# Differential attention in split float32: score matmuls on half the rows of TensorE, and score tiles in pairs of maps

## The chip, the cores and the metric

The kernel runs on one core of one Trainium2 chip. The metric is device time in microseconds (us) for one execution. The engines of the core work at the same time, each through its own instructions in order: TensorE (PE in the profile, PEld its weight loads), VectorE (DVE), ScalarE (ACT), GpSimd (POOL) and SyncE (SP), whose queue issues nearly all DMA transfers here.

## The reference

An encoder layer is applied to two requests, a prompt of 2048 tokens and a sample of 1024, with 1024 features in float32. One big projection gives the inputs of a convolution branch and of an attention branch; the two results are gated, added, projected and normalised. The change touches the attention only:

```python
def diff_attention(q, k, v, lam):            # q, k: (B, S, 4 heads, 2 maps, 64)
    ...
        s = jnp.einsum('bqhcd,bkhcd->bhcqk', q_blk, k).astype(jnp.float32) * scale
        p = jax.nn.softmax(s, axis=-1)
        a = p[:, :, 0] - lam * p[:, :, 1]
        return jnp.einsum('bhqk,bkhe->bqhe', a.astype(v.dtype), v)
```

Each head has two attention maps (c = 0 and 1), each with 64 features for queries and keys. Both go through a softmax, the second is taken from the first with a factor, and the difference multiplies the values.

## The kernel before

The kernel has three stages. Stage A projects and runs the convolution, stage B is the attention, stage C merges and projects. Spills between them go through DRAM.

TensorE's products are made from halves: a float32 number x is kept as a high half, x rounded to the format of the fast matmul (float32r), and a low half, the rest. Stage A writes both halves of queries and keys: `qd[g][h][0]` is high, `[1]` low, and rows 0 to 63 belong to map 0, rows 64 to 127 to map 1. In the names, g is 0 for the prompt and 1 for the sample, h is the head.

In stage B a `Head` (L460) holds the keys of a head in tiles `km[c, hf]` of 128 x 1024: for map c and the half hf of the keys, the high halves on rows 0 to 63 and the low ones on rows 64 to 127. A `Pair` (L476) is 256 queries of a head: 32 pairs in the prompt, 16 in the sample. It loads four query tiles `qq` (L489): for each map the high halves, once on the upper and once on the lower 64 rows, and the low halves in the same way, in eight loads. `score` (L495) makes one PSUM tile `s` of 128 queries (j is 0 or 1) by 1024 keys. It has four matmuls of 512 columns over all 128 rows (L505): the high queries, and then the low ones, against high and low keys together, so all four products of halves are in the sum. The eviction (L507, on VectorE) scales the tile into a buffer `e` and keeps its smallest value. PSUM holds two tiles `s`, two tiles `tp` and two tiles `ops`.

What follows for each j: `soften` (L511) is the exponential of a whole map on ScalarE (L518); `combine` (L521) a reciprocal on VectorE (L524) and three steps on GpSimd (L525 to L527) that bring both maps into one buffer `e`. `turn` (L528 to L537) transposes two blocks of 128 keys for both j, four matmuls into `tp` (L534), and ScalarE rounds them into `ah` (L536). `rest` (L539) takes the low half `al` on VectorE (L541). `product` (L544) makes six matmuls with the values (L95 to L97). After a pair's last product come the squares on ScalarE (`squares`, L551) and, for the pair before, their sum by two matmuls (`sums`, L566).

The order in stage B is written out by hand: TensorE, VectorE, ScalarE and GpSimd take their instructions as the loop at L596 issues them, and only SyncE's order is found by a scheduler. A pass of this loop, a slot below, issues at most one score tile with its eviction, then the turn of an earlier pair, then what stands in the list `mid` for this slot (exponentials, squares), then a product, `al`, and what stands in `late` (combine). So a steady slot on TensorE is four scores, four transposes, six products. A pair of the prompt takes eight slots of scores, and its turns begin eight slots after its last score (`LAGS`); a pair of the sample takes four. The prompt's first two pairs have no turns beside them. Up to `NE` = 8 buffers `e` exist, and `live` counts those in use: a score that needs a new one waits for its slot until the count allows it (L600). Every fourth slot also splits a piece of the weights that stage C keeps resident (L580, L581).

The order of the work in a j before the change is map 0 with both halves of the keys, then map 1 with both halves; the exponential of a map is issued in the slot after its last half.

## Time and profile before

| | |
|---|---|
| Time, median of 3 runs | 2825.17 us (2818.87 to 2825.88) |
| Span of the profiled execution, first to last instruction | 2816.1 us |
| Its own total | not given by the page; the span is 2.8 to 9.8 us under the three runs |
| TensorE busy, matmuls | 2709.3 us (96%), 13818 |
| VectorE, ScalarE, GpSimd busy | 1843.1, 1074.4, 1478.5 us (65%, 38%, 53%) |
| Score matmuls (L505) | 1280, from 1548.0 to 2227.1 us, 352.3 us busy |
| Evictions of scores (L507) | 320, 1.22 or 1.28 us each |

The shares are averages over three stages. Stage B runs from about 1548 to 2230 us, and what the change is worth is read there. In a row of a timeline stand the start, the duration, the engine, the line, the operation, the output and the inputs with their shapes, and how many instructions of a kind the row merges; in brackets the idle time of the engine ahead of it and what ended that. Matmuls overlap in the array, so the duration of a group is longer than its step to the next group. A row of the windows has, after the window and its length, for each engine the busy time and the number of instructions, then the granted clock of TensorE.

### The profile page before, as it was taken

To read this page: it belongs to the slowest core of one execution; us is meant where nothing else is said; L and a number is where in the kernel's file an instruction comes from. 1 tells how busy PE (TensorE), PEld (TensorE's weight loads), DVE (VectorE), ACT (ScalarE), POOL (GpSimd) and SP (SyncE) were. 2 spreads that over 40 slices of the span, in tenths; PEclk is the share of its full clock that TensorE was granted. 3 is DMA by queue.
4 is the path that set the end of the run, shared out by engine and by line. 5 is a ranking of instruction groups with operands and counts; after the bars stand their busy time and mean duration, and the time that the engine had idled before them with its cause. 6 is when DMAs were issued, how large, how long until landed. Compare 5 with 4: busy or idle time off the path is not lost. (4 is left out here: it accounts for less than half of the span.)

```text
span 2816.1 us, 36981 instructions
## 1 busy us (share of the span) xinstructions
PE 2709.3 (96%) x13818; PEld 2274.5 (81%) x13818; DVE 1843.1 (65%) x2564; ACT 1074.4 (38%) x1540; POOL 1478.5 (53%) x774
## 2 busy tenths in 40 slices
PE   9989999998999998979999999999999999999998
PEld 7868988887897877858878788888888877777777
DVE  4961110396387495994940888888888866667665
ACT  3122132212322222213121788878788822222121
POOL 3554232245535424546442899988888833333343
PEclk9999999999999999989999999999999999999999
DMA  6245323324443343334333332322234375566553
GB/s 194 71 152 179 126 105 112 143 72 158 157 142 119 108 138 104 105 127 156 105 116 112 109 85 88 85 69 70 69 94 116 104 253 190 182 207 200 181 162 119
DMA packets 194980, 364.89 MB, mean 130 GB/s; under 512 B 25088, under 2 KB 98288, under 8 KB 194800
## 3 DMA queue, kind: packets, MB, share of 16 engines
q1 hardware_dynamic: 193792, 362.22, 40.1%
q8 instruction: 109, 1.79, 0.3%
q14 instruction: 71, 0.58, 0.1%
q10 hardware_dynamic: 1008, 0.29, 0.1%
HBM read 242.67 MB, written 107.18 MB: 124 GB/s over the span
## 5 line engine op out<-in xcount | busy, mean ns | idle before, releaser
L127 POOL TENSOR_TENSOR wl<-raw,wh 128x1024 fp32r<-128x1024 f32 (+1 forms) x138 | 416.5, 3038 | 485.6 <-ACT wh L126 471.8
L291 PE MATMUL psA<-xh,wh 128*128 128x512 f32 x1920 | 600.6, 395 | 37.7 <-DVE ev L255 16.5
L159 DVE SCALAR_TENSOR_TENSOR acc<-uc,conv_dw,acc 128x512 f32<-128x512 f32 x720 | 608.5, 896 | 5.8
L291 PE MATMUL psA<-xl,wh 128*128 128x512 f32 x1920 | 598.6, 393 | 0.9 <-DVE xl L284 0.9
L291 PE MATMUL psA<-xh,wl 128*128 128x512 f32 x1920 | 597.7, 393 | 0.3 <-POOL wl L127 0.3
L291 PEld LDWEIGHTS psA<-xh,wh 128*128 128x128 f32 x1920 | 365.4, 191 | 116.9 <-DVE ev L255 17.8
L291 PEld LDWEIGHTS psA<-xl,wh 128*128 128x128 f32 x1920 | 365.4, 190 | 78.8 <-DVE xl L284 1.6
L291 PEld LDWEIGHTS psA<-xh,wl 128*128 128x128 f32 x1920 | 364.6, 190 | 77.6 <-POOL wl L127 1.0
L527 POOL TENSOR_TENSOR e<-e 128x2048 f32<-128x2048 f32 (+1 forms) x96 | 373.1, 3887 | 8.0
L505 PE MATMUL s<-km,qq 128*128 128x512 f32 x1280 | 352.3, 397 | 4.8 <-DVE e L507 4.4
L518 ACT ACTIVATE e<-e,mx 128x2048 f32<-128x2048 f32 (+1 forms) x192 | 329.5, 1716 | 1.2 <-DVE e L507 1.1
L507 DVE TENSOR_SCALAR_CACHE_REDUCE e<-s 128x1024 f32<-128x1024 f32 x192 | 233.4, 1216 | 77.1 <-PE s L505 75.7
L541 DVE TENSOR_TENSOR al<-tp,ah 128x512 fp32r<-128x512 f32 x320 | 220.1, 688 | 56.1 <-ACT ah L536 56.1
L505 PEld LDWEIGHTS s<-km,qq 128*128 128x128 f32 x1280 | 219.7, 189 | 41.3 <-DVE e L507 10.7
L126 ACT ACTIVATE wh<-raw 128x1024 fp32r<-128x1024 f32 (+1 forms) x138 | 134.0, 1012 | 285.0 <-PE psA L291 164.9
L536 ACT ACTIVATE ah<-tp 128x512 fp32r<-128x512 f32 x320 | 189.5, 593 | 98.7 <-PE tp L534 96.1
L90 POOL TENSOR_TENSOR zl<-zraw,zh 128x512 fp32r<-128x512 f32 x88 | 123.8, 1409 | 162.4 <-ACT zh L89 142.5
L95 PE MATMUL ops<-ah,vv 128*128 128x256 f32 x640 | 207.3, 324 | 0.2 <-ACT row L567 0.2
L534 PEld LDWEIGHTS tp<-ident,e 128*128 128x128 f32 x1280 | 158.6, 141 | 48.6 <-DVE al L541 3.7
L534 PE MATMUL tp<-ident,e 128*128 128x128 f32 x1280 | 193.3, 274 | 4.5 <-POOL e L527 3.0
L97 PE MATMUL ops<-al,vv 128*128 128x256 f32 x640 | 180.7, 282 | 0.7 <-DVE al L541 0.7
L96 PE MATMUL ops<-ah,vv 128*128 128x256 f32 x640 | 179.7, 281 | 0.0
(165 smaller groups left out, 4259.5 us busy)
## 6 DMA issues: line engine op xcount, KB each, us to landing
raw<-in_w_in SPq DMA_DIRECT2D x130, 512.0 KB
qq<-qd SPq DMA_DIRECT2D x384, 64.0 KB
zraw<-in_w_out SPq DMA_DIRECT2D x88, 256.0 KB
ev<-ev SPq DMA_DIRECT2D x96, 128.0 KB
kd<-ev SPq DMA_DIRECT2D x24, 512.0 KB
qd<-ev SPq DMA_DIRECT2D x24, 512.0 KB
vd<-ev SPq DMA_DIRECT2D x24, 512.0 KB
mcd<-evm SPq DMA_DIRECT2D x24, 512.0 KB
```

Source lines behind the costliest of these rows:

```text
L95: nc.tensor.matmul(ps, ah, bh, start=first, stop=False)
L97: nc.tensor.matmul(ps, ah, bl, start=False, stop=last)
L127: nc.gpsimd.tensor_sub(lo, raw, hi.bitcast(F32))
L159: nc.vector.scalar_tensor_tensor(acc[:, c], src, dw_sb[:, c, k:k + 1], acc[:, c], op0=ALU.mult, op1=ALU.add)
L291: nc.tensor.matmul(ps[:, n * 512:(n + 1) * 512], w[a][:, k, j * P:(j + 1) * P], B.xs[k][x][:, n * 512:(n + 1) * 512], start=k == 0 and a = ...
L505: nc.tensor.matmul(s[:, n * 512:(n + 1) * 512], p.qt[2 * c + i][:, j * P:(j + 1) * P], p.km[c, hf][:, n * 512:(n + 1) * 512], start=i == 0 ...
L507: nc.vector.tensor_scalar(p.e[j, c][:, hf * 1024:(hf + 1) * 1024], s, -SCALE, mx[:, hf - 1:hf] if hf else None, op0=ALU.mult, op1=ALU.min, ...
L518: nc.scalar.activation(e, e, AF.Exp, bias=p.mx[j, c][:, nh - 1:nh], scale=-1.0, accum_out=sc)
L527: nc.gpsimd.tensor_add(e0, e0, e)
L534: nc.tensor.transpose(tp[:, i, j * P:(j + 1) * P], p.e[j, 0][:, kt * P:(kt + 1) * P], ident)
L536: nc.scalar.activation(ah, tp, AF.Copy)
L541: nc.vector.tensor_sub(al, tp, ah.bitcast(F32))
```

## The change

The product of low queries and low keys is left out of the scores. The high queries still multiply high and low keys in one matmul over 128 rows. The low queries of both maps now lie in one tile `ql`, map 0 on rows 0 to 63 and map 1 on rows 64 to 127, and multiply the high keys only, in matmuls over 64 rows each. For that the keys of map 1 are loaded with the halves swapped, so that their high halves lie on rows 64 to 127. A pair's queries come in five loads instead of eight.

```diff
     # Head
-                            nc.sync.dma_start(kk.bitcast(F32)[i * HD:(i + 1) * HD], kd[g][h][i, c * HD:(c + 1) * HD, r])
+                            d = (i ^ c) * HD
+                            nc.sync.dma_start(kk.bitcast(F32)[d:d + HD], kd[g][h][i, c * HD:(c + 1) * HD, r])
     # Pair.load
-                self.qt = []
+                q = slice(self.qp * 256, self.qp * 256 + 256)
+                self.qh = []
                 for c in range(2):
-                    for i in range(2):
-                        qq = kvp.tile([P, 256], F32R, name=f"qq{c}{i}", bufs=2)
...
+                    qq = kvp.tile([P, 256], F32R, name=f"qq{c}", bufs=2)
+                    for r in range(2):
+                        nc.sync.dma_start(qq.bitcast(F32)[r * HD:(r + 1) * HD, :], qd[self.g][self.h][0, c * HD:(c + 1) * HD, q])
+                    self.qh.append(qq)
+                self.ql = kvp.tile([P, 256], F32R, name="ql", bufs=2)
+                nc.sync.dma_start(self.ql.bitcast(F32), qd[self.g][self.h][1, :, q])
     # score
-            s = psS.tile([P, 1024], F32, name="s")
-            for n in range(2):
-                for i in range(2):
-                    nc.tensor.matmul(s[:, n * 512:(n + 1) * 512], p.qt[2 * c + i][:, j * P:(j + 1) * P],
-                                     p.km[c, hf][:, n * 512:(n + 1) * 512], start=i == 0, stop=i == 1)
-            nc.vector.tensor_scalar(p.e[j, c][:, hf * 1024:(hf + 1) * 1024], s, -SCALE,
...
+            if c == 0:
+                p.s = []
+            p.s.append(psS.tile([P, 1024], F32, name="s"))
+            q = slice(j * P, (j + 1) * P)
+            ns = [slice(n * 512, (n + 1) * 512) for n in range(2)]
+            for n in ns:
+                nc.tensor.matmul(p.s[c][:, n], p.qh[c][:, q], p.km[c, hf][:, n], start=True, stop=False)
+            if c == 0:
+                return
+            for n in ns:
                 for i in range(2):
+                    r = slice(i * HD, (i + 1) * HD)
+                    nc.tensor.matmul(p.s[i][:, n], p.ql[r, q], p.km[i, hf][r, n], start=False, stop=True)
+            for i in range(2):
+                mx = p.mx[j, i]
+                nc.vector.tensor_scalar(p.e[j, i][:, hf * 1024:(hf + 1) * 1024], p.s[i], -SCALE,
...
     # the order of the scores, and the slots of the exponentials
-            todo += [(p, j, c, hf) for j in range(2) for c in range(2) for hf in range(p.L // 1024)]
+            todo += [(p, j, c, hf) for j in range(2) for hf in range(p.L // 1024) for c in range(2)]
-                if todo and (todo[0][3] or live[0] < NE):
+                if todo and (todo[0][3] or todo[0][2] or live[0] + todo[0][0].L // 1024 <= NE):
-                    if hf == p.L // 1024 - 1:
-                        def f(p=p, j=j, c=c, now=now):
+                    if c == 1 and hf == p.L // 1024 - 1:
+                        for i in range(2):
+                            def f(p=p, j=j, c=i, now=now + i):
...
-                        mid[now + 1].append(f)
+                            mid[now + 1 + i].append(f)
```

Two score tiles, one of each map, now belong together. The slot of map 0 issues two matmuls and no eviction; the slot of map 1 issues two matmuls, four on half the rows, and both evictions. The exponentials of a j are issued in the two slots after its last scores, one map in each.

On TensorE, this is a slot of the prompt's thirteenth pair before (map 1, second half of the keys for j = 0: `s` are score tiles, `km` keys, `qq` queries, `tp` transposes of `e`):

```order
L505 MATMUL s_12682<-km_11445,qq10_12370 128x512
L505 MATMUL s_12682<-km_11445,qq11_12373 128x512
L505 MATMUL s_12682<-km_11445,qq10_12370 128x512
L505 MATMUL s_12682<-km_11445,qq11_12373 128x512
L534 MATMUL tp_12688<-ident_65,e_12149 128x128
L534 MATMUL tp_12688<-ident_65,e_12258 128x128
L534 MATMUL tp_12688<-ident_65,e_12149 128x128
L534 MATMUL tp_12688<-ident_65,e_12258 128x128
```

And this is a slot of map 1 in the same pair after it (slot 6 of its eight; `s_12657` was begun in the slot before):

```order
L511 MATMUL s_12680<-km_11406,qq1_12318 128x512 x2
L517 MATMUL s_12657<-km_11403,ql_12321 128x512
L517 MATMUL s_12680<-km_11406,ql_12321 128x512
L517 MATMUL s_12657<-km_11403,ql_12321 128x512
L517 MATMUL s_12680<-km_11406,ql_12321 128x512
L547 MATMUL tp_12689<-ident_65,e_12100 128x128
L547 MATMUL tp_12689<-ident_65,e_12209 128x128
L547 MATMUL tp_12689<-ident_65,e_12100 128x128
L547 MATMUL tp_12689<-ident_65,e_12209 128x128
```

The tile of map 0 is finished by the third of the four half matmuls, two rows ahead of the transposes.

On VectorE, two slots of that pair before have an eviction (from `s` to `e`) and an `al` each:

```order
L507 TENSOR_SCALAR e_12712,mx_12713<-s_12714 128x1024
L541 TENSOR_TENSOR al_12737<-tp_12720,ah_12725 128x512
L507 TENSOR_SCALAR e_12712,mx_12713<-s_12739,mx_12713 128x1024
L541 TENSOR_TENSOR al_12758<-tp_12745,ah_12750 128x512
L524 RECIPROCAL cc_12760<-ssum_12729 128x1
```

After it the evictions come in twos, and so do the `al`; these are slots 6 to 8 of the pair, where `e_12678` takes over the buffer that `e_12100` had, the `e` whose last transposes go into `tp_12709`:

```order
L520 TENSOR_SCALAR e_12655,mx_12656<-s_12657 128x1024
L520 TENSOR_SCALAR e_12678,mx_12679<-s_12680 128x1024
L554 TENSOR_TENSOR al_12704<-tp_12689,ah_12694 128x512
L554 TENSOR_TENSOR al_12726<-tp_12709,ah_12714 128x512
L537 RECIPROCAL cc_12728<-ssum_12696 128x1
L520 TENSOR_SCALAR e_12655,mx_12656<-s_12706,mx_12656 128x1024
L520 TENSOR_SCALAR e_12678,mx_12679<-s_12733,mx_12679 128x1024
```

The eviction into `e_12678` stands ahead of the `al` of `tp_12709`, and it waits on TensorE for the transposes of that tile which read `e_12100`.

On ScalarE, the exponentials (from `e` to `e`) of one j before, with what stands between them:

```order
L518 ACTIVATE e_12603,stats_10076<-e_12603,mx_12604 128x2048
L536 ACTIVATE ah_12693<-tp_12688 128x512
L580 ACTIVATE w_attn_oh_10082<-wraw_12589 128x256
L567 ACTIVATE row_12707<-ops_12414 1x256
L536 ACTIVATE ah_12725<-tp_12720 128x512
L557 ACTIVATE sq_12727<-ot_12670,kscale_321 128x256
L518 ACTIVATE e_12655,ssum_12729<-e_12655,mx_12656 128x2048
```

And after it:

```order
L570 ACTIVATE sq_12667<-ot_12606,kscale_321 128x256
L531 ACTIVATE e_12546,stats_10076<-e_12546,mx_12547 128x2048
L549 ACTIVATE ah_12694<-tp_12689 128x512
L531 ACTIVATE e_12567,ssum_12696<-e_12567,mx_12568 128x2048
L549 ACTIVATE ah_12714<-tp_12709 128x512
```

The second exponential follows the first with one `ah` between them, where two of them and three other instructions stood before.

SyncE's queue, whose order the scheduler finds, now has the first head's keys and queries between stage A's last spills of the values and its last weight loads; before they stood behind the weight loads.

More of the change, by code (lines that the diff above doesn't have):

```diff
@@ L485, in load @@
                 self.km, self.vv = head.km, head.vv
-                self.qt = []
+                q = slice(self.qp * 256, self.qp * 256 + 256)
+                self.qh = []
                 for c in range(2):
-                    for i in range(2):
-                        qq = kvp.tile([P, 256], F32R, name=f"qq{c}{i}", bufs=2)
-                        for r in range(2):
-                            nc.sync.dma_start(qq.bitcast(F32)[r * HD:(r + 1) * HD, :],
-                                              qd[self.g][self.h][i, c * HD:(c + 1) * HD, self.qp * 256:self.qp * 256 + 256])
-                        self.qt.append(qq)
+                    qq = kvp.tile([P, 256], F32R, name=f"qq{c}", bufs=2)
[4 more added lines that the diff above has]
+                nc.sync.dma_start(self.ql.bitcast(F32), qd[self.g][self.h][1, :, q])
         def score(p, j, c, hf):
@@ L500, in score @@
                 p.mx[j, c] = sm.tile([P, 2], F32, name="mx")
-            mx = p.mx[j, c]
-            s = psS.tile([P, 1024], F32, name="s")
-            for n in range(2):
-                for i in range(2):
-                    nc.tensor.matmul(s[:, n * 512:(n + 1) * 512], p.qt[2 * c + i][:, j * P:(j + 1) * P],
-                                     p.km[c, hf][:, n * 512:(n + 1) * 512], start=i == 0, stop=i == 1)
-            nc.vector.tensor_scalar(p.e[j, c][:, hf * 1024:(hf + 1) * 1024], s, -SCALE,
-                                    mx[:, hf - 1:hf] if hf else None, op0=ALU.mult, op1=ALU.min,
-                                    accum_out=mx[:, hf:hf + 1])
+            if c == 0:
[8 more added lines that the diff above has]
+            for n in ns:
+                for i in range(2):
+                    r = slice(i * HD, (i + 1) * HD)
[3 more added lines that the diff above has]
+                nc.vector.tensor_scalar(p.e[j, i][:, hf * 1024:(hf + 1) * 1024], p.s[i], -SCALE,
+                                        mx[:, hf - 1:hf] if hf else None, op0=ALU.mult, op1=ALU.min,
+                                        accum_out=mx[:, hf:hf + 1])
         def soften(p, j, c):
@@ L612, in encoder_kernel, with f @@
                         p.at = now + p.lag
-                    if hf == p.L // 1024 - 1:
-                        def f(p=p, j=j, c=c, now=now):
-                            sc = soften(p, j, c)
-                            if c == 1:
-                                def f():
-                                    combine(p, j, sc)
-                                    live[0] -= p.L == 2048
-                                late[now + 2].append(f)
-                        mid[now + 1].append(f)
+                    if c == 1 and hf == p.L // 1024 - 1:
+                        for i in range(2):
+                            def f(p=p, j=j, c=i, now=now + i):
+                                sc = soften(p, j, c)
+                                if c == 1:
+                                    def f():
+                                        combine(p, j, sc)
+                                        live[0] -= p.L == 2048
+                                    late[now + 2].append(f)
+                            mid[now + 1 + i].append(f)
                 for again in range(2):
```

## Prediction

> **What bounds the kernel now.** I read the page first, then the busy time by windows, then the timelines of the attention stage, the only stage that the change touches. The page:
>
> ```profile
> span 2816.1 us, 36981 instructions
> PE 2709.3 (96%) x13818; PEld 2274.5 (81%) x13818; DVE 1843.1 (65%) x2564; ACT 1074.4 (38%) x1540; POOL 1478.5 (53%) x774
> ```
>
> TensorE is busy nearly all the time, so what it is spared counts, as long as nothing else ends last in that stage. The windows (busy us of PE, PEld, DVE, ACT, POOL, then the granted clock) and the wait of the scores for DVE in the stage (us in total, times, longest):
>
> ```profile
> 1700.00:1900.00 200.00, 200.00 (x1352) 177.98 (x1351) 177.59 (x308) 165.72 (x253) 182.79 (x98) 1.00 0.29 82
> PE s L505 <- DVE e L507: 4.4, 9, 2.1
> ```
>
> TensorE never stands still there, and it waits for an eviction only 4.4 us in the whole stage. But DVE is at 89% and POOL at 91%: a TensorE quicker by a tenth would meet both. The TensorE timeline gives the price of a slot, and the sums of squares, two matmuls once per 256 queries, mark the period (first and last of them, and between them the row that counts 48 of their weight loads, so 24 marks):
>
> ```profile
> 1700.95 0.28 PE L566 MATMUL ops<-sqh,ones 128*1 128x256 f32 x1
> ...
> 1702.12 0.60 PE L534 MATMUL tp<-ident,e 128*128 128x128 f32 x4
> 1702.47 0.36 PE L95 MATMUL ops<-ah,vv 128*128 128x256 f32 x1
> ...
> 1703.27 1.07 PE L505 MATMUL s<-km,qq 128*128 128x512 f32 x4
> 1704.18 0.60 PE L534 MATMUL tp<-ident,e 128*128 128x128 f32 x4
> ...
> 2089.65 0.28 PE L566 MATMUL ops<-sqh,ones 128*1 128x256 f32 x1
> ```
>
> ```profile
> 1700.90:2089.70 388.80, 9.29 (x47) 3.84 (x48) 1.00 0.27 78
> ```
>
> A slot is scores 0.91 us (1703.27 to 1704.18, so 0.23 a matmul), transposes 0.35, products 0.80. Eight slots with one sum take (2089.65 - 1700.95) / 23 = 16.90 us.
>
> **What the change saves on TensorE.** Two slots (call them A for map 0, B for map 1) hold 8 full score matmuls now; afterwards 4 full ones and 4 on 64 rows. The latter are built for rows 0 to 63 and 64 to 127 with different PSUM banks. No row of this trace shows two matmuls sharing the array, so the second of each couple costs between 0 (it rides along) and 0.23 us. I take 0: nothing that the couple uses is shared. Then two slots lose 2 x 0.23 = 0.46 us of TensorE, and eight slots would need 16.90 - 1.82 = 15.08 us. The Trainium skill (TensorE: Matmul & The Clock Gate, Part 3, measured speedup) has four 32-row tiles run 3.07 times as fast together; by that the sum keeps the zero, and without it the sum is that of the third rival. No run here shows it yet.
>
> **What it adds: a wait for the eviction.** There are two score tiles in PSUM. Now they alternate, and each has a slot in which to be emptied. Afterwards the tile of map 0 is finished only in slot B, by the third of the four half matmuls, and the next slot A overwrites it. Behind that matmul stand the transposes and products of slot B, and in-order TensorE does nothing else. The rows for this loop are a score and its eviction where DVE was idle, and scores that had to wait for an eviction, at the stage's start:
>
> ```profile
> 2153.61 1.09 PE L505 MATMUL s<-km,qq 128*128 128x512 f32 x4
> ```
>
> ```profile
> 2154.74 1.22 DVE L507 TENSOR_SCALAR_CACHE_REDUCE e<-s 128x1024 f32<-128x1024 f32 x1 [0.25 <-PE s L505]
> ```
>
> ```profile
> 1548.04 1.08 PE L505 MATMUL s<-km,qq 128*128 128x512 f32 x4
> ...
> 1557.70 1.23 DVE L507 TENSOR_SCALAR_CACHE_REDUCE e<-s 128x1024 f32<-128x1024 f32 x1
> ...
> 1558.98 1.20 PE L505 MATMUL s<-km,qq 128*128 128x512 f32 x4 [0.59 <-DVE e L507]
> 1559.06 1.28 DVE L507 TENSOR_SCALAR_CACHE_REDUCE e<-s,mx 128x1024 f32<-128x1024 f32 x1
> ...
> 1560.40 2.34 PE L505 MATMUL s<-km,qq 128*128 128x512 f32 x8 [0.22 <-DVE e L507]
> ...
> 1572.52 0.90 PE L534 MATMUL tp<-ident,e 128*128 128x128 f32 x3 [3.01 <-POOL e L527]
> ```
>
> From the start of four score matmuls to the eviction is 1.13 us; the third half matmul starts where the fourth full one did, so I keep 1.13. From the eviction's start to the waiting scores is 1.28 us (first half of the keys) or 1.34 (second half). After the wait the four matmuls take 1.20 us, not 1.09: 0.11 for weights not loaded ahead. So from B to the next A it is 2.41 or 2.47 us, where TensorE's own work is 0.91 + 0.35 + 0.80 = 2.06. From A to B: 0.46 + 0.11 + 0.35 + 0.80 = 1.72. The loop is 4.13 or 4.19 us, and four loops are 16.64. The wait eats nearly the whole saving, 0.26 us of 1.82 is left, and the sum of squares, which stands at the end of a B slot, hides in the wait.
>
> **Three delays on that loop.** They come from DVE's and ScalarE's queues. Their rows:
>
> ```profile
> 1706.27 0.69 DVE L541 TENSOR_TENSOR al<-tp,ah 128x512 fp32r<-128x512 f32 x1 [0.60 <-ACT ah L536]
> 1706.88 0.15 DVE L524 RECIPROCAL cc<-ssum 128x1 f32<-128x1 f32 x1
> 1706.95 1.21 DVE L507 TENSOR_SCALAR_CACHE_REDUCE e<-s 128x1024 f32<-128x1024 f32 x1
> ...
> 1708.08 0.68 DVE L541 TENSOR_TENSOR al<-tp,ah 128x512 fp32r<-128x512 f32 x1
> ```
>
> ```profile
> 1703.28 0.49 ACT L557 ACTIVATE sq<-ot,kscale 128x256 f32<-128x256 f32 x1
> 1703.68 1.99 ACT L518 ACTIVATE e<-e,mx 128x2048 f32<-128x2048 f32 x1
> ...
> 1705.67 0.57 ACT L536 ACTIVATE ah<-tp 128x512 fp32r<-128x512 f32 x1
> ...
> 1706.90 0.60 ACT L536 ACTIVATE ah<-tp 128x512 fp32r<-128x512 f32 x1 [0.66 <-PE tp L534]
> 1707.39 0.41 ACT L89 ACTIVATE sqh<-sq 128x256 fp32r<-128x256 f32 x1
> 1707.70 2.01 ACT L518 ACTIVATE e<-e,mx 128x2048 f32<-128x2048 f32 x1
> ...
> 1709.69 0.59 ACT L536 ACTIVATE ah<-tp 128x512 fp32r<-128x512 f32 x1
> ```
>
> ```profile
> 1706.26 0.60 PE L534 MATMUL tp<-ident,e 128*128 128x128 f32 x4
> ```
>
> Steps from start to start: transposes to `ah` 0.64 (1706.26 to 1706.90), `ah` to the next 0.49, an exponential to the next 1.99 (1707.70 to 1709.69), `ah` to `al` 0.60 (1705.67 to 1706.27), `al` 0.61 (1706.27 to 1706.88), the reciprocal 0.07, an eviction to the next operation 1.13 (1706.95 to 1708.08).
>
> First, the exponentials of both maps now stand in neighbouring slots (1 and 2, 5 and 6), and every third slot's `ah` is behind both. From the score start of slot 8: slot 1 at 2.47, its transposes 3.04, its `ah` 3.68, exponential 4.17, slot 2's `ah` 6.16, exponential 6.65, slot 3's `ah` 8.64, its `al` 9.24, the reciprocal 9.85, and DVE is free at 9.92. TensorE reaches slot 2 at 4.19 and slot 4 at 8.32, so slot 4's first eviction is due at 9.45: 0.47 late, and the next scores wait for that eviction.
>
> Second, the buffer of `e`. In the built program the first eviction of map 1 in slot 6 takes the buffer that the pair before last frees with its last transposes, which stand in slot 7. They start at 7.17 from the score start of slot 4, the third of them, the one waited for, ends at about 7.68 (0.60 less one step of 0.09), the eviction starts at 7.72, and slot 8, which needs its PSUM tile, at 9.00 instead of 8.32: 0.68 late. Behind the waiting eviction on DVE are slot 6's and slot 7's `al`.
>
> Third, slot 8's first eviction, due at 10.13: ScalarE's chain as above with the squares' 0.40 (1703.28 to 1703.68) ahead frees DVE at 10.32, 0.19 late.
>
> Eight slots: 16.64 + 0.47 + 0.68 + 0.19 = 17.98 us, 1.08 more than 16.90. The prompt has 32 such pairs; the first two fill the pipeline. 30 x 1.08 = 32 us.
>
> **Start, sample, loads.** At the start no transposes lie between the scores. A loop is then 1.13 + 0.11 + 1.15 + 1.28 = 3.7 us, as slot B waits for the second eviction too; the first eviction is at 1548.04 + 0.46 + 1.13 = 1549.6, the eighth 7 x 3.7 later at 1575.5, and the first transposes at about 1575.3, where now the second ones come at 1572.52: 3 us. In the sample's stage POOL sets the pace and before it the prompt's POOL work is close behind:
>
> ```profile
> 1699.80 0.21 POOL L525 TENSOR_TENSOR cc<-cc,stats 128x1 f32<-128x1 f32 x1
> ...
> 1707.53 0.20 POOL L525 TENSOR_TENSOR cc<-cc,stats 128x1 f32<-128x1 f32 x1
> ...
> 1715.27 0.75 POOL L581 TENSOR_TENSOR w_attn_ol<-wraw,w_attn_oh 128x256 fp32r<-128x256 f32 x1
> 1715.96 0.20 POOL L525 TENSOR_TENSOR cc<-cc,stats 128x1 f32<-128x1 f32 x1
> ...
> 2150.05 0.20 POOL L525 TENSOR_TENSOR cc<-cc,stats 128x1 f32<-128x1 f32 x1
> ...
> 2158.64 0.20 POOL L525 TENSOR_TENSOR cc<-cc,stats 128x1 f32<-128x1 f32 x1
> ```
>
> In the prompt eight slots need 7.73 + 8.43 = 16.16 us of POOL, and 14.7 once the resident weights (two of 0.75) are split: below 17.98, no bound. In the sample four slots need 8.59 us (2150.05 to 2158.64), and two loops 8.26 hide under that: 0.
>
> The loads: 144 fewer of 64 KB. The first keys and queries are issued earlier, into a gap of SyncE's queue in the projection stage:
>
> ```profile
> 1384.47 6.24 SPq L250 DMA_DIRECT2D mcd<-evm  x2
> ...
> 1410.14 2.71 SPq L114 DMA_DIRECT2D raw<-in_w_in  x2
> ...
> 1492.12 2.42 SPq L469 DMA_DIRECT2D km<-kd  x4
> ```
>
> Four loads of keys take 2.42 us to issue, so the first eight take 4.8 and the queries' ten at that pace 6, in a gap of 19 us (1390.71 to 1410.14); only the next head's four (2.4 us) can push a weight load. I put this at nothing; 2.4 us if that cover is gone.
>
> **The sum.** 32 + 3 = 35 us on the span of 2816.1. The page gives no total for that execution; the median is 9 us above the span, and I carry the difference over: 2825.17 + 35 = 2860 us.
>
> **The rivals.** One, no change: the exponentials and the buffer of `e` cost nothing, since in time they come free earlier than my chain says. Then 30 x -0.26 + 3 = -5, so 2820 us; for it, each delay is under 0.7 us; against it, the buffer's wait is in the program.
>
> Two, faster: the eviction ends in time, and TensorE works through. It decides at 2.06 us from B to the next A, and the rows give 2.41. If so, POOL's 16.16 bounds the first half (15 x 0.74) and TensorE's 15.08 the rest (15 x 1.82): 38 us less, 2787.
>
> Three, the halves run one after the other: the third starts 0.23 later, 120 loops, 28 us more: 2888. For it, no row shows sharing; against it, they use different rows and banks.
>
> Four, the array has to empty before it takes 64-row work. A score matmul lasts 0.38 us (1.07 less three steps of 0.23), 0.15 beyond its step, so each loop is 0.15 longer, 120 x 0.15 = 18 us more: 2878. For it, the full matmuls stand directly ahead of the halves; against it, no row of before shows such a change. The Trainium skill (TensorEngine Tiling, Key Properties) says that changing the tiling mode drains TensorE; by that rule this rival holds, and no row here bears it out yet.
>
> **How the numbers follow.** Forecast 0.50, rival one 0.09, two 0.06, three 0.20, four 0.15. Differences under 0.3% (8.5 us) can't be told from none here. Faster 0.06, same 0.09 (rival one), slower 0.85. The range starts at 2833, where the second and third delays are gone (30 x 0.87 less), and ends at 2900, rival three with most of rival four's price; it leaves out the first two rivals and little else.
>
> **What would show it.** Right: TensorE waits for DVE's eviction before half of the score groups, in all some 70 us (30 x (17.98 - 15.08), less the late weights), in place of 4.4; a pair's period near 18.0; half matmuls that start together; DVE waiting once per pair for the transposes. Wrong: a period below 16.9, TensorE still at 100% in that stage, or half matmuls 0.23 us apart.

## The result, and the profile after

The changed kernel takes 2888.24 us (median of 4 runs, 2886.75 to 2892.07), the kernel before, beside it on the same chip, 2823.98 (4 runs, 2818.87 to 2825.88): the ratio is 1.0237, with a 95% interval of 1.0223 to 1.0252. That is 64 us, where the forecast had 35: the sign and the range held, the size did not. The median of a run below leaves out an execution in a slower state.

The page after, its span and its line of the engines:

```profile
span 2887.1 us, 36774 instructions
PE 2745.9 (95%) x13818; PEld 2204.1 (76%) x13818; DVE 1840.2 (64%) x2564; ACT 1075.8 (37%) x1540; POOL 1481.6 (51%) x774
```

TensorE issues as many matmuls as before and is still the busiest engine, but its share fell. The span is 71.0 us longer than that of the profiled execution before; the medians differ by 64, because the profiled execution before lies 7.9 us under its median and the one after 1.1 under its own. The marks between the pairs, the first matmul of each sum of squares, show where. First before, then after: the 29 marks from the prompt's first pair on, and a run of the sample's (duration in ns: least, median, most; then the first and the last start).

```profile
L566 PE MATMUL ops<-sqh,ones x29: 279/279/279, 1616.5 to 2089.7; 128*1 128x256 f32 x29
L566 PE MATMUL ops<-sqh,ones x10: 279/279/279, 2149.2 to 2226.2; 128*1 128x256 f32 x10
```

```profile
L579 PE MATMUL ops<-sqh,ones x29: 279/279/279, 1635.0 to 2152.8; 128*1 128x256 f32 x29
L579 PE MATMUL ops<-sqh,ones x15: 279/279/279, 1895.2 to 2152.8; 128*1 128x256 f32 x15
L579 PE MATMUL ops<-sqh,ones x8: 279/279/279, 2232.6 to 2295.0; 128*1 128x256 f32 x8
```

The first mark is 18.5 us late. The 28 periods behind it take 517.8 us, not 473.2: 44.6 more. Undisturbed, a period is (2152.8 - 1895.2) / 14 = 18.40 us, where 17.98 was forecast; the mean of all 28 is 18.49. A sample pair takes (2295.0 - 2232.6) / 7 = 8.91 us, not (2226.2 - 2149.2) / 9 = 8.56. From the last mark shown here (three more of the prompt follow) to the end 7.9 us are added, about half of it the sample's. 18.5 + 44.6 + 7.9 = 71.0.

One undisturbed prompt pair after, on TensorE (start, time, then what ended an idle time); of the slots only the full score matmuls are shown, A and B in turn from the first row on, and of the first B its halves and transposes too:

```profile
1932.32 0.73 PE L511 MATMUL s<-km,qq 128*128 128x512 f32 x2
...
1934.03 0.63 PE L511 MATMUL s<-km,qq 128*128 128x512 f32 x2
1934.59 0.73 PE L517 MATMUL s<-km,ql 64*128 64x512 f32 x4
1935.25 0.66 PE L547 MATMUL tp<-ident,e 128*128 128x128 f32 x4
...
1936.74 0.73 PE L511 MATMUL s<-km,qq 128*128 128x512 f32 x2
...
1939.12 0.73 PE L511 MATMUL s<-km,qq 128*128 128x512 f32 x2 [0.50 <-DVE e L520]
...
1941.90 0.74 PE L511 MATMUL s<-km,qq 128*128 128x512 f32 x2
...
1943.62 0.63 PE L511 MATMUL s<-km,qq 128*128 128x512 f32 x2
...
1946.23 0.73 PE L511 MATMUL s<-km,qq 128*128 128x512 f32 x2
...
1947.95 0.63 PE L511 MATMUL s<-km,qq 128*128 128x512 f32 x2
...
1950.70 0.73 PE L511 MATMUL s<-km,qq 128*128 128x512 f32 x2
```

From A to B it is 1.71, 2.38, 1.72 and 1.72 us, 7.53 in all (forecast 7.56, with the one late by the buffer of `e`). From B to the next A it is 2.71, 2.78, 2.61 and 2.75, 10.85 in all, where the forecast had 10.42. DVE's evictions in the same pair:

```profile
1935.45 1.22 DVE L520 TENSOR_SCALAR_CACHE_REDUCE e<-s 128x1024 f32<-128x1024 f32 x1 [0.61 <-PE s L517]
1937.84 1.23 DVE L520 TENSOR_SCALAR_CACHE_REDUCE e<-s 128x1024 f32<-128x1024 f32 x1 [1.15 <-PE tp L547]
...
1944.94 1.23 DVE L520 TENSOR_SCALAR_CACHE_REDUCE e<-s 128x1024 f32<-128x1024 f32 x1 [0.51 <-PE s L517]
...
1949.30 0.15 DVE L537 RECIPROCAL cc<-ssum 128x1 f32<-128x1 f32 x1
1949.37 1.27 DVE L520 TENSOR_SCALAR_CACHE_REDUCE e<-s,mx 128x1024 f32<-128x1024 f32 x1
```

An idle DVE gets a tile 1.32 us (1943.62 to 1944.94) or 1.42 us (1934.03 to 1935.45) behind the start of slot B's scores, not 1.13. The halves do run together: a view of 1934.585 to 1934.600 alone has the first two of them,

```profile
1934.59 0.50 PE L517 MATMUL s<-km,ql 64*128 64x512 f32 x2
```

and all four with the step to the transposes take 0.66 us (1934.59 to 1935.25). But the full matmuls take 0.56 to the halves (1934.03 to 1934.59), not 0.46, and the halves 0.20 more than two rides of 0.23. In the trace the third and the fourth half start at 1934.93, 0.89 us behind the first full matmul of the slot; the forecast had the third at three steps of 0.23, 0.69.

The waits of the whole execution (us in total, times, longest):

```profile
PEld s L511 <- DVE e L520: 86.6, 193, 3.3
...
PEld s L517 <- issue: 60.9, 160, 0.7
...
DVE e L520 <- PE tp L547: 34.6, 30, 1.2
...
PE s L511 <- DVE e L520: 32.2, 47, 3.1
```

TensorE, with its weight loads, now waits for the eviction. The second row says that in every couple the load of the halves' weights waits some 0.38 us for nothing that the profile shows, which would fit an array that takes the new shape only when it is empty; no run here looks into that.

### The profile page after: what moved, and what is told of

The parts are those of the page before. It is cut to its first block, busy times and chain, and to the rows that moved or that the text cites. A ratio compares the mean times of both kernels' runs of the same rounds, so it can differ in the third digit from the quotient of the medians.

```text
span 2887.1 us, 36774 instructions
## 1 busy us (share of the span) xinstructions
PE 2745.9 (95%) x13818; PEld 2204.1 (76%) x13818; DVE 1840.2 (64%) x2564; ACT 1075.8 (37%) x1540; POOL 1481.6 (51%) x774
## 5 line engine op out<-in xcount | busy, mean ns | idle before, releaser
L291 PEld LDWEIGHTS psA<-xh,wh 128*128 128x128 f32 x1920 | 365.4, 191 | 116.8 <-DVE ev L255 18.5
L511 PE MATMUL s<-km,qq 128*128 128x512 f32 x640 | 228.3, 439 | 40.7 <-DVE e L520 32.2
L547 PEld LDWEIGHTS tp<-ident,e 128*128 128x128 f32 x1280 | 147.1, 141 | 80.7 <-issue 28.2
L547 PE MATMUL tp<-ident,e 128*128 128x128 f32 x1280 | 201.9, 280 | 1.7 <-DVE al L554 1.5
L539 POOL TENSOR_SCALAR e<-e,cc,neglam 128x2048 f32<-128x2048 f32 (+1 forms) x96 | 170.8, 1779 | 10.0
```

The costliest lines, as they stand in the source:

```text
L291: nc.tensor.matmul(ps[:, n * 512:(n + 1) * 512], w[a][:, k, j * P:(j + 1) * P], B.xs[k][x][:, n * 512:(n + 1) * 512], start=k == 0 and a = ...
L511: nc.tensor.matmul(p.s[c][:, n], p.qh[c][:, q], p.km[c, hf][:, n], start=True, stop=False)
L547: nc.tensor.transpose(tp[:, i, j * P:(j + 1) * P], p.e[j, 0][:, kt * P:(kt + 1) * P], ident)
```

## Experiments: what do 64 rows cost?

Two theories. "Emptying": going from 128-row to 64-row work and back costs TensorE time (the fourth rival's mechanism, here on top of the forecast's loop). "Queues": 64 rows cost nothing, and the forecast's delays of ScalarE, DVE and the buffer of `e` were too small.

**full_rows.** The halves on all rows.

```
-            for n in ns:
-                for i in range(2):
-                    r = slice(i * HD, (i + 1) * HD)
-                    nc.tensor.matmul(p.s[i][:, n], p.ql[r, q], p.km[i, hf][r, n], start=False, stop=True)
+            for i in range(2):
+                for n in ns:
+                    nc.tensor.matmul(p.s[i][:, n], p.ql[:, q], p.km[i, hf][:, n], start=False, stop=True)
```

> Slot B's four half matmuls become four on all 128 rows (map 0's two first, so that the eviction's operand is complete after the same four matmuls as the forecast had it); they add the low queries of one map times the low keys of the other to each score. Theory 'emptying' (the 64-row group costs TensorE about 0.10 us ahead and 0.20 us behind, and delays the eviction by 0.30 us): these prices go. TensorE's slot B is then 6 x 0.23 + 0.35 + 0.80 = 2.53 us, the eviction is due 2.41 us after B's start, a pair's period is 16.9 plus what is left of the three delays, about 17.9 in place of 18.45, and the time about 30 x 0.55 = 16 us under the changed kernel's 2888, so 2872. Theory 'queues' (64-row work costs nothing, the forecast's delays from ScalarE and the buffer of e are only larger than worked out): slot B gets 0.12 us longer and nothing shorter, the period 18.45 + 4 x 0.12 = 18.9, the time 2902.

Measured: 2861.85 us, 1.0141 times the kernel before (1.0119 to 1.0163), 26 us under the changed kernel. Its marks in the prompt's second half:

```profile
L578 PE MATMUL ops<-sqh,ones x13: 279/279/279, 1911.6 to 2128.7; 128*1 128x256 f32 x13
```

The period is (2128.7 - 1911.6) / 12 = 18.09. With twice the matmul rows in slot B the kernel is quicker: "queues" is out. The prompt gave 28 x 0.3 = 9 us of the 26; most of the rest is the start of the stage (first mark at 1619.8, 15 us earlier), below. Of these 15 us 4.9 stand ahead of the first scores (1545.10 against 1550.04), which the halves don't touch.

**halves_alone.** The kernel before, with each slot's two low matmuls on 64 rows, unpaired.

```
-            for n in range(2):
-                for i in range(2):
-                    nc.tensor.matmul(s[:, n * 512:(n + 1) * 512], p.qt[2 * c + i][:, j * P:(j + 1) * P],
-                                     p.km[c, hf][:, n * 512:(n + 1) * 512], start=i == 0, stop=i == 1)
+            for i in range(2):
+                r = slice(0, HD if i else P)
+                for n in range(2):
+                    nc.tensor.matmul(s[:, n * 512:(n + 1) * 512], p.qt[2 * c + i][r, j * P:(j + 1) * P],
+                                     p.km[c, hf][r, n * 512:(n + 1) * 512], start=i == 0, stop=i == 1)
```

> The kernel before, with its own order and its eviction per slot, but each slot's two low matmuls on 64 rows only (low queries times high keys), behind the two full ones, with no partner to ride along. Theory 'emptying': each of the eight slots pays about 0.3 us, a prompt pair's period is 16.90 + 8 x 0.3 = 19.3 us, a sample pair's 8.55 + 1.2, the time 2824 + 32 x 2.4 + 16 x 1.2 = 2920. Theory 'queues': 64 rows cost what 128 rows cost, the period stays 16.90 and the time 2824 within 0.3%. The scores' group from its start to the transposes would be 0.91 us by 'queues' and 1.2 by 'emptying'.

Measured: 2921.55 us, ratio 1.0352 (1.0328 to 1.0377). Its marks, and two slots of its TensorE:

```profile
L567 PE MATMUL ops<-sqh,ones x15: 279/279/279, 1900.3 to 2175.4; 128*1 128x256 f32 x15
```

```profile
1900.52 1.29 PE L506 MATMUL s<-km,qq 128*128 128x512 f32 x4
1901.74 0.66 PE L535 MATMUL tp<-ident,e 128*128 128x128 f32 x4
1902.95 1.29 PE L506 MATMUL s<-km,qq 128*128 128x512 f32 x4
```

Scores to transposes take 1.22 us, not 0.91, the slot 2.43, the period 19.65: (19.65 - 16.90) / 8 = 0.34 us per slot, for half the rows in two of four matmuls and no wait at all. And a paired slot B after the change also takes 0.56 + 0.66 = 1.22 from its full matmuls to the transposes, with four halves in it, not two: the second map's halves ride along at no cost, as forecast.

**halves_mixed.** The same with `n` outside and `i` inside again, so that full and half alternate.

> As halves_alone, but each slot's four score matmuls in the order of the kernel before: full, half, full, half. The work is the same, TensorE goes into 64-row work and out of it twice a slot, not once. 'Emptying' (a price for each change of the rows in use, 0.34 us per change there and back in halves_alone): 2 x 0.34 = 0.69 per slot, a pair's period 16.90 + 8 x 0.69 = 22.4 in place of 19.65, the time about 2823 + 32 x 5.5 + 16 x 2.2 = 3030. Rival (64-row matmuls are slower or load their weights later, at a fixed price for each): the same two of them, the same 19.65 and 2921.

Measured: 3058.13 us, ratio 1.0823 (1.0786 to 1.0859). Its marks in the prompt:

```profile
L567 PE MATMUL ops<-sqh,ones x18: 279/279/279, 1903.5 to 2290.2; 128*1 128x256 f32 x18
```

The period is (2290.2 - 1903.5) / 17 = 22.75, so 0.73 us per slot: the same two halves, twice the changes, twice the price. So the price goes with the changes and is not a fixed one per 64-row matmul. Within a trip it is spread: in the trace of halves_alone the starts are 0.23 us apart between the full matmuls, 0.33 from full to half, 0.34 from half to half, and 0.32 from the last half to the transposes. The Trainium skill (TensorEngine Tiling (Array Packing), Key Properties) says that a change of the tiling mode drains TensorE and gives no price; by that rule the price is paid per change, and halves_alone and halves_mixed agree, with 0.34 us in and out.

## Experiments: the cover of the eviction

**both_in_b.** Map 0's full matmuls move from slot A to slot B, so that slot A's transposes and products stand between the halves and the next scores.

```
             if c == 0:
-                p.s = []
-            p.s.append(psS.tile([P, 1024], F32, name="s"))
...
-            for n in ns:
-                nc.tensor.matmul(p.s[c][:, n], p.qh[c][:, q], p.km[c, hf][:, n], start=True, stop=False)
-            if c == 0:
                 return
+            p.s = [psS.tile([P, 1024], F32, name="s") for _ in range(2)]
...
+            for i in range(2):
+                for n in ns:
+                    nc.tensor.matmul(p.s[i][:, n], p.qh[i][:, q], p.km[i, hf][:, n], start=True, stop=False)
```

> The changed kernel with map 0's two full score matmuls moved from slot A to slot B, directly ahead of map 1's: the transposes and products of slot A then stand between slot B's halves and the next scores, about 1.15 us more cover for the eviction. Theory 'eviction wait' (TensorE's wait for the tile of map 0 is what turned the saving into a loss): that wait goes, a couple takes TensorE's own 0.46 + 0.56 + 0.66 + 1.15 + 1.15 = 3.98 us, four of them and the sums 16.2, GpSimd's 16.16 lies just under it, and the buffer of e adds some 0.2: period 16.2 to 16.8 in place of 18.45, time about 2888 - 29 x 1.85 = 2834. Rival 'queues': the exponentials in neighbouring slots and the buffer of e hold the loop whatever TensorE's order is; the period stays above 17.9 and the time above 2870.

Measured: 2841.77 us, ratio 1.0084 (1.0068 to 1.0100), 46 us under the changed kernel. Its marks in the two halves of the prompt, and an undisturbed couple:

```profile
L578 PE MATMUL ops<-sqh,ones x13: 276/279/279, 1630.2 to 1844.5; 128*1 128x256 f32 x13
L578 PE MATMUL ops<-sqh,ones x14: 279/279/279, 1895.6 to 2113.7; 128*1 128x256 f32 x14
```

```profile
2006.14 1.08 PE L512 MATMUL s<-km,qq 128*128 128x512 f32 x4
2007.15 0.73 PE L516 MATMUL s<-km,ql 64*128 64x512 f32 x4
2007.82 0.66 PE L546 MATMUL tp<-ident,e 128*128 128x128 f32 x4
...
2010.18 1.08 PE L512 MATMUL s<-km,qq 128*128 128x512 f32 x4
```

The wait for the eviction was the main loss. With most of it gone the period is 16.78 in the second half, under the 16.90 of before, and 17.86 in the first, where the resident weights are split and ScalarE waits for their single raw buffer. The edit does not change the cover alone: DVE's wait for the transposes, the second delay, falls too, from 31.1 us in 27 waits to 7.5 in 25 (1640 to 2140 us). By e9_clean below that delay is worth 0.43 us a pair, about a quarter of the 1.62 that the second half gains. The couple takes 4.04 us of TensorE, so 4 x 4.04 + 0.23 = 16.39 per pair would be its own: of the 1.82 us that the prediction wanted to save, the changes of shape leave 0.51.

**b_full.** The same order, halves on all rows as in full_rows.

> As both_in_b, with the halves on all 128 rows as in full_rows: TensorE has the work of the kernel before (eight full score matmuls in a couple), the paired evictions, but neither 64-row work nor the short cover. 'Eviction wait': 0.46 + 0.46 + 0.92 + 1.15 + 1.15 = 4.14 us per couple, period 16.8, time that of the kernel before plus the start of the stage, 2823 to 2830; so the 39 us by which full_rows is above the kernel before are the wait's. 'Queues': the pairing itself costs them, 2862.

Measured: 2845.34 us, ratio 1.0094 (1.0079 to 1.0110). That is 17 us under full_rows for the same move, but still above the kernel before, and its period in the second half is 17.13 (first 17.8). In the first half ScalarE waits for the raw buffer of the weights again (26.9 us from 1640 to 2140). But the second is 0.23 over the kernel before too, so the pairing costs something beside the cover, perhaps by evictions, `al` and exponentials that come in twos; no run takes that apart. The expectation of 2830 at most was 15 us too low.

## Experiments: the three delays

**lag7.** `LAGS = (8, 8)` becomes `(7, 8)`.

> The changed kernel with a prompt pair's transposes one slot earlier: the buffer of e that slot 6's second eviction takes is then freed by slot 6's own transposes, ahead of the eviction, and no longer by slot 7's. By the forecast's second delay (0.68 us per pair) 30 x 0.68 = 20 us go, and one slot (2 us) at the stage's end: 2866. Rival: the next delay (al behind ah behind the exponentials) is late by as much, and nothing goes: 2886 to 2888. In the trace the evictions that wait for transposes (34.6 us, 30 times) should be gone in both cases.

Measured: 2895.40 us, ratio 1.0254 (1.0234 to 1.0275): nothing gained. Its waits in the prompt (1640 to 2140 us):

```profile
PEld tp L547 <- POOL e L540: 17.5, 26, 1.0
PEld ops L579 <- ACT ot L566: 16.6, 26, 1.2
...
DVE e L520 <- PE tp L547: 1.0, 1, 1.0
```

The eviction's wait is gone, as expected, but a slot less between scores and turn is a slot that GpSimd's combination needed: the transposes now wait for it once a pair, and the sum of squares for `ot`. The period is 18.86. The run moved the wait rather than removed it, so it doesn't size the delay.

**exp_apart.** `now=now + 2 * i` and `mid[now + 1 + 2 * i]` in place of `i`.

> The changed kernel with the second exponential of a couple two slots behind the first, not one, and its combination on GpSimd one slot later. By the forecast's first and third delay (0.47 + 0.19 us per pair) 30 x 0.66 = 20 us go: 2868. Rival: slot 6's eviction, which waits for the transposes, holds the loop anyway, or the later combination holds a buffer of e longer: 2888 or more. In the trace DVE's waits for ah (37.8 us, 56 times, longest 1.4) should shrink to under half in both cases.

Measured: 2899.15 us, ratio 1.0266 (1.0244 to 1.0287). Its waits in the same stretch:

```profile
PEld tp L547 <- POOL e L540: 20.0, 27, 0.8
...
DVE al L554 <- ACT ah L549: 11.6, 27, 0.5
```

The waits for `ah` fell (from 24.4 us in the same stretch of the changed kernel to 11.6), and the time did not: the later combination is waited for in its place, and the delay that was to go was hardly there any more (see the three delays in the account of the prediction).

**e9.** A ninth buffer of `e`; to make room, two buffers of `ah` and `al`, not three, one buffer of the last stage's factors `rb`, not two, and two constants moved into stage A's memory (the last not shown).

```
-        ap_ = pool(name="b_at", bufs=3)
+        ap_ = pool(name="b_at", bufs=2)
...
-        ep = pool(name="b_e", bufs=NE)
+        ep = pool(name="b_e", bufs=NE + 1)
...
-                loaded.append([cin.tile([P, 512], F32, name=n, bufs=2) for n in
+                loaded.append([cin.tile([P, 512], F32, name=n, bufs=1 if n == "rb" else 2) for n in
```

> The changed kernel with nine buffers of e for the same gating of the scores (room made by two in place of three buffers of ah and al, two constants moved into the projection stage, and one buffer in place of two for the last stage's factors, which may add a few us there). No eviction then waits for transposes (34.6 us in 30 waits go to 0). By the forecast's second delay a pair's period falls by 0.68, 18.45 to 17.8, and the time by about 19 us to 2869. Rival: another queue is late by as much, and the period stays 18.4 and the time 2888.

Measured: 2928.90 us, ratio 1.0392 (1.0371 to 1.0412), because of the room I made, as its waits show:

```profile
ACT ah L551 <- PE ops L93: 179.0, 157, 2.3
```

A product stands two slots behind its `ah`, so two buffers are one too few. The run says nothing on `e`.

**e9_clean.** The ninth buffer again, three of `ah` and `al`, five of the values in place of six; `rb` stays single, and the two constants stay moved.

> The changed kernel with nine buffers of e for the same gating, as e9, but with the three buffers of ah and al kept (in e9 ScalarE's ah waited 179 us, 157 times, for the products that free them, which hid what was asked). Room comes from five in place of six buffers of values, two constants moved into the projection stage and one buffer of the last stage's factors. No eviction waits for transposes. By the forecast's second delay (1.72 to 2.38 us from A to B in slots 7 and 8) the period falls by 0.66 from 18.4 to 17.75, the time by 19 us to 2869, or a few more for the last stage. Rival: the loop has another delay of that size behind it (al behind ah behind the exponentials, GpSimd's combination), and the period stays above 18.2, the time 2883 or more.

Measured: 2887.19 us, ratio 1.0236 (1.0219 to 1.0254): no change in all, but a gain and a loss behind it. Its marks in the prompt, then a wait that the changed kernel has not:

```profile
L581 PE MATMUL ops<-sqh,ones x14: 276/279/279, 1901.0 to 2134.6; 128*1 128x256 f32 x14
```

```profile
DVE x L433 <- DMA rb<-rrd: 29.5, 16, 3.8
```

The period is 17.97, and no eviction waits for transposes any more, so the buffer of `e` costs 0.43 us a pair (forecast 0.68), 12 us over 28 periods. Its last mark stands at 2313.7, 18.5 us ahead of the changed kernel's 2332.2; 7.4 of these are there at the first mark already (1627.6 against 1635.0), and nothing here says why. From the last mark to the end of its span of 2879.9 it takes 566 us, the changed kernel 2887.1 - 2332.2 = 555. So the single buffer `rb` of the last stage takes 11 of them back. The profiled execution is also the quickest of this run, 5.5 us under its median.

## Experiment: the start of the stage

TensorE at the start of the changed kernel's attention stage, and the window behind it (busy us of PE, PEld, DVE, ACT, POOL, then the granted clock):

```profile
1563.73 2.36 PE L511 MATMUL s<-km,qq 128*128 128x512 f32 x4 [1.32 <-DVE e L520]
1566.02 1.22 PE L517 MATMUL s<-km,ql 64*128 64x512 f32 x4
1568.62 2.42 PE L511 MATMUL s<-km,qq 128*128 128x512 f32 x4 [1.38 <-DVE e L520]
```

```profile
1560.00:1575.00 15.00, 10.97 (x26) 4.84 (x26) 7.40 (x14) 8.71 (x11) 7.67 (x5) 0.50 0.51 132
```

A loop takes 4.89 us, not the forecast's 3.7, and the halves 1.22, not 0.73: the granted clock is 0.50. In full_rows, where TensorE has work for two more full matmuls per loop, the loop there is 3.72 and the clock 1.00:

```profile
1556.59 0.73 PE L511 MATMUL s<-km,qq 128*128 128x512 f32 x2 [0.86 <-DVE e L519]
...
1560.31 0.73 PE L511 MATMUL s<-km,qq 128*128 128x512 f32 x2 [0.92 <-DVE e L519]
```

The kernel before showed such a clock in the same place, and the prediction did not use it: behind the standstill of 3.01 us that it quotes, four score matmuls take 2.07 us and not 1.09, and from 1572.5 to 1577.5 the granted clock is 0.50.

```profile
1573.28 2.07 PE L505 MATMUL s<-km,qq 128*128 128x512 f32 x4
```

**warm_start.** Work for TensorE in that time.

```
                     score(p, j, c, hf)
+                    if now <= 16 and c == 1:
+                        tp = psT.tile([P, 512], F32, name="tp")
+                        for i in range(4):
+                            nc.tensor.matmul(tp, p.qh[0][:, :P], p.km[0, hf][:, :512], start=True, stop=True)
```

> The changed kernel with four extra full matmuls, whose result nobody reads, behind the halves of each of the first eight couples, where TensorE has no transposes yet and waits 1.3 to 1.4 us twice a loop. Theory 'clock': the granted clock of 0.50 between 1557 and 1590 us comes from TensorE standing still there; kept busy, it gets 0.8 or more, a loop takes under 4.2 us in place of 4.9, the first transposes start near 1578 in place of 1587, and the time falls by about 9 us to 2879. Rival: the loop is long for another reason (64-row work, the loads of that time); the clock or the loop stays, and the time is 2888 to 2896.

Measured: 2879.64 us, ratio 1.0217 (1.0202 to 1.0232). The same window, and the first mark:

```profile
1560.00:1575.00 15.00, 12.37 (x48) 5.90 (x46) 9.68 (x18) 9.19 (x13) 11.83 (x7) 1.00 0.43 112
```

```profile
L579 PE MATMUL ops<-sqh,ones x1: 279/279/279, 1625.9 to 1625.9; 128*1 128x256 f32 x1
```

More work, and less time: the clock is 1.00, the first mark comes at 1625.9 and not at 1635.0, 9.1 us earlier, and the span is 8.0 shorter. Of the 9.1 us 1.1 stand ahead of the first scores (1548.91 against 1550.04), so 8.0 are the start's. The intervals of the two ratios overlap, so these 8 us stand on the traces. The Trainium skill (TensorE: Matmul & The Clock Gate, Part 1, what's actually happening) puts the half rate behind an idle window of about 3.4 us. The trace agrees on the half, but shows no standstill of that length: no wait in this start is over 1.42 us.

## Experiments: a version without these losses

**b_best**, from both_in_b: nine buffers of `e` as in e9_clean; the first two pairs scored map by map; the resident weights' step moved.

```
+            single = p in pairs[:2]
-            if c == 0:
+            if c == 0 and not single:
                 return
+            maps = [c] if single else [0, 1]
...
-                if now % 4 == 0:
+                if now % 4 == 2:
                     next(pieces, None)
```

> both_in_b with three causes of its remaining waits taken away: nine buffers of e (as e9_clean); the first two pairs scored one map at a time, each with its own halves and eviction, so that the start of the stage has no paired wait and TensorE's clock no reason to fall; and the resident weights' step two slots earlier, ahead of GpSimd's combination and not behind it, so that ScalarE does not wait for the single raw buffer (36 us between 1600 and 1900 us in both_in_b, 7 in the kernel before). Then TensorE's own 4 x 4.04 + 0.23 = 16.39 us per pair should bound, 0.5 under the kernel before: 30 x 0.5 = 15 us less, and 3 us more for sample and last stage: about 2810 where the kernel before has 2823. Rival: GpSimd's 16.16 and DVE's queue do not fit that closely, the period stays at 16.8 to 17.0, and the time 2820 to 2830.

Measured: 2845.31 us, ratio 1.0092 (1.0075 to 1.0108). Its marks in the prompt's two halves:

```profile
L582 PE MATMUL ops<-sqh,ones x13: 279/279/279, 1621.1 to 1829.1; 128*1 128x256 f32 x13
L582 PE MATMUL ops<-sqh,ones x15: 279/279/279, 1862.9 to 2097.1; 128*1 128x256 f32 x15
```

The periods are (1829.1 - 1621.1) / 12 = 17.33 and (2097.1 - 1862.9) / 14 = 16.73: in the second half about the rival's 16.8. The time is above the expectation's 2810 and above the rival's 2820 to 2830. The last mark of all, at 2275.7, is 18 us earlier than in both_in_b, and the single `rb` takes 17 of them back behind it (568 us from there to the end, not 551; spans of 2843.5 and 2844.7).

**b_last**: `rb` in two buffers, four of the values, the step at `now % 4 == 3`.

> b_best with the last stage's factors in two buffers again (its one buffer cost DVE 24 us of waits for DMA there; the last stage took 568 us from the last sum of squares to the end of the span, the kernel before takes 551), the room taken from the buffers of values (four), and the resident weights' step one slot later, clear of the exponentials on ScalarE. If that buffer was the whole of b_best's surplus, 17 us go and the attention stage keeps its 11 us over the kernel before: 2829 or less. If the prompt's first half (period 17.34 in b_best, 16.72 in the second) was held by the step's place on ScalarE, it falls to 16.8 and the time to 2821, the kernel before's within 0.3%. Rival: four buffers of values hold up the loads at the three changes of the prompt's head, 1 to 3 us each, and the time is 2832 or more.

Measured: 2816.85 us (12 runs) where the kernel before has 2821.49 (17 runs): ratio 0.9985 (0.9973 to 0.9998). Its marks in the whole prompt:

```profile
L582 PE MATMUL ops<-sqh,ones x29: 276/279/279, 1621.8 to 2090.1; 128*1 128x256 f32 x29
```

Now the period is 16.73 all through, 0.17 under the kernel before. Of the three edits only the step's place concerns ScalarE in the prompt, so it most likely had held the first half; it was not moved alone. With two buffers of `rb` the time from the last mark to the end is 552 us again. But the first mark is 5 us late, and a sample pair takes 8.69 ((2230.0 - 2160.5) / 8), not 8.56. The whole is 0.15% under the kernel before, less than the 0.3% that the prediction counts as a difference: with most of the losses removed that were found, the change is worth next to nothing here.

## Why the prediction was right in sign and short in size

- **What bounds, what is saved.** Right: the halves ride along at no cost. But the price of a change of shape, 0.34 us per couple, was not in the sum, and takes 1.4 of the saved 1.82 us per pair. It had been left to the fourth rival, at 0.15 per loop.
- **The eviction's wait.** Right in mechanism, and the main loss: both_in_b took 46 us off by more cover, the shorter wait for the buffer of `e` included. Its size: from B to the next A 2.71, 2.78, 2.61, 2.75 us, where the forecast's bare loops are 2.41 or 2.47. The failed step is "the third half matmul starts where the fourth full one did, so I keep 1.13": the third half starts 0.89 us behind the first full matmul, not 0.69, and it is 1.32 to 1.42 to the eviction, 0.19 to 0.29 more.
- **The three delays.** They were added to the loop, and a delay only counts where the loop is not late already. With 0.20 to 0.31 more in each of the four loops (1.09 in all), the first and third delay (0.66) have hardly anything left: the eviction of slot 4 starts 1.42 us behind its scores, as slot 6's does with DVE idle, and slot 8's finds DVE idle. 1.09 - 0.66 = 0.43 is the difference of 10.85 and 10.42. The second delay was there in full (2.38 in place of 1.72), though its removal gave 0.43 of 0.68. So 18.38 in place of 17.98, by two errors of opposite sign. Over the 28 periods: 12 us more than forecast, and 2.6 for the few longer periods, whose cause I did not try.
- **The start.** 3 us forecast, 18.5 measured, of which 2.0 stand ahead of the first scores (1550.04 against 1548.04). The step that failed is the loop of 3.7: it holds at full clock (3.72 in full_rows), and the clock was taken for granted. warm_start gives 8 of the other 13.5 back; no run takes the rest apart.
- **The sample.** "Two loops 8.26 hide under that" (GpSimd's 8.59) failed with the loop, where B to A takes 2.61 us here too (2250.70 to 2253.31), and by a sum of squares that stands at the end of an A slot, so that no wait hides its 0.24: 2 x (1.72 + 2.61) + 0.24 = 8.90, measured 8.91, some 4 us in all.
- **Loads.** In the prompt, from 1640 to 2140 us, TensorE waits for none.
- **The rivals.** One and two are out. Three is out: the halves start together; that its 2888 us are the measured time to the microsecond is chance. Four is what happened, on top of the forecast's loop as it had said, with 0.20 to 0.31 per loop where it had 0.15. 12 + 2.6 + 15.5 + 4 us more than the forecast's 35 make 69 of the 71 us of the spans; the rest lies in the last stage, where single profiles differ by a few us. The spans themselves differ by 7 us more than the medians, so a few of these microseconds belong to the two executions and not to the change.

## What to carry to other kernels

Before packing small matmuls, count the changes of shape as well as the rows: here each trip in and out cost 0.34 us, as much as one and a half full matmuls, and that ate three quarters of the saving. An instruction that finishes two tiles at once also finishes the first one late: look at what stands between it and the next writer of that tile, because moving two matmuls behind work that was there anyway was worth more (46 us) than a ninth buffer of `e` (12 us of the prompt). And the delays found on one loop did not add: two of the three vanished behind a loop that was late already, so take a maximum per place before you sum.

## What the runs showed of the hardware

- A change from 128-row to 64-row matmuls and back: 0.34 us per trip (halves_alone), 0.73 for two (halves_mixed); two groups on different rows run at the price of one (1.22 us from scores to transposes with two halves or with four; the two start together at 1934.59).
- TensorE's granted clock fell to 0.50 with no idle stretch over 1.42 us, when it had six full matmuls' time of work in a loop of about 4 us (the changed kernel and both_in_b); with eight (full_rows, b_full), or six and four extra (warm_start), it was 1.00 in the same 15 us. Where between these it falls was not tried.
